# Decay casts on VectorE, half-out projections that open operand by operand, and held blocks evacuated one by one

## The chip, the cores and the metric

The kernel runs on one core of one Trainium2 chip. The metric is the device time of one execution in microseconds (us). The core's engines run side by side, each through its own row of instructions in order, and wait for each other by semaphores: TensorE (PE, matmuls; PEld, its weight loads), VectorE (DVE), ScalarE (ACT), GpSimd (POOL), and SyncE (SP), which issues the loads. [...]

## The reference

Three transformer blocks are applied in sequence to one input x of 512 positions and 1024 features, all in fp32. Cut to what matters here:

```python
x = first_block(x, ...)    # norm, mLSTM and differential attention, out projection, FFN, gated PLE, norm
x = second_block(x, ...)   # stick_breaking_layer, then mla_layer
x = third_block(x, c, ...) # swiglu, hybrid_mixer, swiglu; each modulated by c

# first block
x = x + mixed @ w_out
# second block
return x + (o * jax.nn.silu(gate)) @ w_out       # stick breaking: l0_w_out
# third block
mod = (jax.nn.silu(c) @ w_ada[l] + b_ada[l]).reshape(b_, N_SUB, 3, D_MODEL)
h = modulate(x, norm_pre_g[l, 0], shift[:, 0], scale[:, 0])
h = swiglu(h, ffn_w_gate[l, 0], ffn_w_up[l, 0], ffn_w_down[l, 0])
x = x + 0.5 * (1 + gate[:, 0, None, :]) * rms_norm_3(h, norm_post_g[l, 0])
```

The mLSTM's gates give cumulated decays, in rows of 4 heads by 512 positions. The hybrid mixer's forgetting attention has a cumulated log gate as well, in rows of 8 heads (cs below).

## The kernel before

All activations are held feature-major, as eight tiles X of 128 features by 512 positions. A matmul's fp32 operands are split into a high part (a cast to fp32r: hi, or wh for a weight) and a low part (lo, wl: the value less the high part), and a product is three matmuls: hi with wh, lo with wh, hi with wl. For a weight, load() issues a DMA of 128x1024 into one of three raw buffers, ScalarE casts wh and VectorE subtracts wl. A projection of one 128-feature block over 1024 features, in proj() and mm(), is 24 matmuls of 128x512 into one PSUM bank (tile pm).

The order of the instructions on each engine is decided when the kernel is built, by a scheduler with a cost model; the code's own order is its input. TensorE is in order like the others.

Five places matter here.

*Decays.* In the first block, decays(sb) makes, for each of the four 128-position blocks, a cumulated gate G, a column tile cc and a split tile R of the range from that block to the end, 512 to 128 columns wide. The split is made by parts(): a MEMSET of the tile, the high part in one group of rows (L408, a cast by ScalarE) and the low part in another (L409, VectorE). The calls for the last two blocks stand in the code behind values("w1_mv"), whose projections are token-major matmuls of 128x256 (mm_tok, L439 to L441), evicted by ScalarE as tiles vt (L816). columns() then transposes the four cc on TensorE (tile cps). In the hybrid mixer the same parts() splits cs, which TensorE multiplies into cumb (L1624).

*Half-out projections.* out_half() projects eight blocks and adds half of each to X; it is called with w_out1 in the first block (403 to 452 us) and with w_l0o in the stick-breaking layer (1161 to 1210 us). Here each block is a proj(), and the column sum of the next norm follows at the end.

*Lead.* lead() opens several banks at once: for each operand k, it issues the three matmuls of every bank. The blocks are left in self.ready, from where proj() takes them. The kernel before uses it at the head of other stages, in two halves of 256 columns each.

*Background steps.* The third block's modulation vector is made in 72 steps; each loads a 128x1024 weight into a raw buffer (adaw) and reduces it by one VectorE operation (L1403). proj() starts one at every second call that it counts:

```python
        if (name, i) in self.ready:
            return self.ready.pop((name, i))
        self.count += 1
        if self.count % 2 == 0:
            self.background()
```

ada_finish(), at the end of the mla layer, ahead of its output projection w_l1o, issues all that are left.

*Held blocks.* out_units() makes an output projection of eight blocks, two to a unit. With held=2 the last two units are held back: their banks are made in two turns, for the columns 0 to 255 and 256 to 511, so that a turn's norm (column sum, rc on GpSimd, broadcast bc) can run beside the other turn's matmuls. A bank pm holds two blocks of 256 columns, c = 0 and 1. evac is what takes a block out: in the mla X gets half of it added (L1363, VectorE); in a swiglu's second half H gets it added (L1495, VectorE); in the hybrid mixer ScalarE copies it (L1665). Each then squares it (sq, ScalarE, L254) and sums the squares (acc, VectorE, L258), and the column sum (colsum, L560) reads acc. Four stages end so: the mla, the two swiglus and the hybrid mixer.

Of the kernel before, what the change touches and what calls it, by code (L numbers as in the profile page):

```python
# [20 lines left out]
ALL = slice(0, S)  # L21
# [265 lines left out]
class Net:  # L287
# [116 lines left out]
    def parts(self, out, src, n, sl=ALL):  # L404

        nc = self.nc
        nc.vector.memset(out.bitcast(F32)[:, sl], 0.0)
        nc.scalar.copy(out[0:n, sl], src[0:n, sl])  # L408
        nc.vector.tensor_tensor(out[64:64 + n, sl], src[0:n, sl], out[0:n, sl].bitcast(F32), ALU.subtract)  # L409

    def load(self, name, u, kc, g):
# [74 lines left out]
    def out_units(self, units, x, evac, held=0, turn=None, ahead=None, skip=0):  # L486


        def part(w, j, c, o, sl, n):
            wj, kc = w  # L490
            xs = [(h[:, sl], l[:, sl]) for h, l in x[4 * j:4 * j + kc]]
            self.mm(o, wj, c * P, xs, start=j == 0, stop=j == n - 1)

        def load(piece):
            name, i, kc = piece
            return self.load(name, i, kc, 256), kc

        n = len(units) - held
        two = range(skip, skip + 2) if n - skip >= 2 else range(0)
        if two:  # L500
            J = len(units[skip])
            self.wide, wide = True, self.wide
            ps = {}
            for js in (range(J - 1), range(J - 1, J)):
                for u in two:
                    ws = {j: load(units[u][j]) for j in js}
                    for c in range(2):
                        if (u, c) not in ps:
                            ps[u, c] = self.psm()
                        for j in js:  # L510
                            part(ws[j], j, c, ps[u, c], ALL, J)
                        if J - 1 in js:
                            evac(2 * u + c, ps[u, c], ALL)
            self.wide = wide
        for u in range(skip + len(two), n):
            w = [load(p) for p in units[u]]
            for c in range(2):
                ps = self.psm()
                for j in range(len(w)):
                    part(w[j], j, c, ps, ALL, len(w))  # L520
                evac(2 * u + c, ps, ALL)
        if held == 0:
            return
        ws = [[load(p) for p in units[u]] for u in range(n, n + held)]
        for th, sl in enumerate(HALVES):
            for a, w in enumerate(ws):
                ps = self.psm()
                for c in range(2):
                    for j in range(len(w)):
                        part(w[j], j, c, ps[:, 256 * c:256 * c + 256], sl, len(w))  # L530
                for c in range(2):
                    evac(2 * (n + a) + c, ps[:, 256 * c:256 * c + 256], sl)
            turn(th)
            if ahead is not None and th == 0:
                with self.tc.issue_after(self.dve.ins):
                    ahead()
# [509 lines left out]

    def out_half(self, name, y, norm=None):

        for i in range(8):
            ps = self.proj(name, i, y)  # L1050
            self.nc.vector.scalar_tensor_tensor(self.X[i], ps, 0.5, self.X[i], ALU.mult, ALU.add)
            if norm is not None:
                norm.add(i, self.X[i])
# [382 lines left out]
    def turn(self, s, H, hn, th, nxt, x, done):  # L1436

        nc, sl = self.nc, HALVES[th]
        n = S // 2
        rb = hn.rows(sl, "po")[:, :n]  # L1440
        for k in range(8):
            h, X = H[k][:, sl], self.X[k][:, sl]
            nc.vector.scalar_tensor_tensor(h, h, self.P3[:, 8 * s + k:8 * s + k + 1], rb, ALU.mult, ALU.mult)  # L1443
            if k % 2:
                nc.gpsimd.tensor_tensor(X, X, h, ALU.add)
            else:
                self.dve = nc.vector.tensor_tensor(X, X, h, ALU.add)
            if nxt is not None:
                nxt.add_pe(k, self.X[k], sl)
            else:  # L1450
                done(k, sl)
        if nxt is not None:
            self.enter(s + 1, nxt, th, x)
# [358 lines left out]
```

## Time and profile before

| | us |
|---|---|
| median of 3 runs | 2478.08 |
| lowest and highest of them | 2474.18, 2478.57 |
| the profiled execution's own time | 2473.0 |
| its span, first to last instruction | 2471.1 |
| TensorE busy in the span | 2406.2 (97%) |
| VectorE busy | 1324.0 (54%) |
| ScalarE busy | 991.8 (40%) |
| GpSimd busy | 64.2 (3%) |

Busy time of TensorE is the modelled time of its matmuls. The span lies 1.9 us under the execution's time; what is outside it is start and end. The mean granted clock is 0.989. The DMA queues moved 240.77 MB, 97 GB/s over the span. In the profile's rows, "idle before <- X" means that the engine stood still before the instruction and that X ended last of what it waited for.

### The profile page before, as it was taken

Reading aid. Unit: us, or ns where it says so; the run is one execution under the profiler, and the core shown is the slowest. Engines: PE = TensorE matmul, PEld = TensorE weight load, DVE = VectorE, ACT = ScalarE, POOL = GpSimd, SP = SyncE. Lnnn points to the kernel's source line nnn. Section 1 sums busy time; section 2 is a strip of 40 time slices with the busy share of each in tenths; the row PEclk is TensorE's granted clock in tenths of the full one; section 3 lists DMA queues with packets and bytes.
Section 4 is the critical chain, followed back from the end, with each engine's and each line's share of the span. In section 5 each row is a group of like instructions: output and inputs, shape, how many; then the busy total and the mean of one; then the engine's idle time right before and its main releaser. Section 6 shows DMA issues by size and latency. Waiting matters only on the chain. (4 is left out here: it accounts for less than half of the span.)

```text
span 2471.1 us, 31023 instructions
## 1 busy us (share of the span) xinstructions
PE 2406.2 (97%) x12462; PEld 1980.4 (80%) x12462; DVE 1324.0 (54%) x2240; ACT 991.8 (40%) x1579; POOL 64.2 (3%) x62
## 2 busy tenths in 40 slices
PE   8999999999999999999999999999999999999998
PEld 6877778888888787777877798888898768888887
DVE  7536557684675664446556863323364565432333
ACT  5423433442343545665334643232245444322221
POOL 0000000000000000000000000000010002000001
PEclk9999999999999999999999999999999999999999
DMA  5223235433433432222301323232222211223221
GB/s 190 94 91 98 90 103 179 136 126 105 160 118 115 136 113 76 69 77 77 115 20 63 109 88 111 88 105 98 86 77 78 90 36 60 94 88 109 94 94 44
DMA packets 71745, 240.77 MB, mean 97 GB/s; under 512 B 8232, under 2 KB 11184, under 8 KB 71600
## 3 DMA queue, kind: packets, MB, share of 16 engines
q1 hardware_dynamic: 71600, 238.78, 29.3%
q8 instruction: 98, 1.61, 0.3%
q14 instruction: 47, 0.39, 0.0%
HBM read 236.64 MB, written 2.11 MB: 97 GB/s over the span
## 5 line engine op out<-in xcount | busy, mean ns | idle before, releaser
L429 PE MATMUL pm<-hi,wh 128*128 128x512 f32 (+1 forms) x2736 | 1043.4, 382 | 8.5 <-ACT hi L393 4.7
L430 PE MATMUL pm<-lo,wh 128*128 128x512 f32 (+1 forms) x2736 | 1041.4, 381 | 0.5 <-DVE lo L394 0.4
L431 PE MATMUL pm<-hi,wl 128*128 128x512 f32 (+1 forms) x2736 | 1039.0, 380 | 0.0
L419 ACT CAST wh<-raw 128x1024 fp32r<-128x1024 f32 (+1 forms) x372 | 381.8, 1029 | 781.5 <-PE pm L430 536.2
L420 DVE TENSOR_TENSOR wl<-raw,wh 128x1024 fp32r<-128x1024 f32 (+1 forms) x372 | 445.3, 1197 | 442.2 <-ACT wh L419 417.5
L429 PEld LDWEIGHTS pm<-hi,wh 128*128 128x128 f32 x2736 | 516.2, 189 | 108.4 <-issue 7.9
L430 PEld LDWEIGHTS pm<-lo,wh 128*128 128x128 f32 x2736 | 516.2, 189 | 97.6 <-issue 3.7
L431 PEld LDWEIGHTS pm<-hi,wl 128*128 128x128 f32 x2736 | 516.1, 189 | 96.1 <-issue 3.0
L439 PE MATMUL pm<-wh,hi 128*128 128x256 f32 x400 | 115.7, 289 | 4.9 <-ACT vt L816 4.9
L1403 DVE CUSTOM_DVE_ANT_0 adaw<-adaw,cb 128x1024 f32<-128x1024 f32 x72 | 87.9, 1221 | 54.2 <-DMA adaw<-in_w_ada 54.1
L441 PE MATMUL pm<-wh,lo 128*128 128x256 f32 x400 | 114.4, 286 | 0.0
L440 PE MATMUL pm<-wl,hi 128*128 128x256 f32 x400 | 114.0, 285 | 0.0
L1482 DVE TENSOR_TENSOR sg<-sg,pm 128x512 f32<-128x512 f32 x44 | 30.2, 687 | 133.3 <-PE pm L431 133.3
L572 POOL TENSOR_TENSOR rc<-ms,nhalf 128x4 f32<-128x4 f32 (+2 forms) x29 | 39.3, 1356 | 2309.6 <-DVE ms L577 1863.8
L439 PEld LDWEIGHTS pm<-wh,hi 128*128 128x128 f32 x400 | 77.6, 194 | 5.9 <-ACT vt L816 5.4
L440 PEld LDWEIGHTS pm<-wl,hi 128*128 128x128 f32 x400 | 77.6, 194 | 0.6 <-issue 0.2
L441 PEld LDWEIGHTS pm<-wh,lo 128*128 128x128 f32 x400 | 77.5, 194 | 0.2
L970 DVE SCALAR_TENSOR_TENSOR uy<-ur,vec,uy 128x511 f32<-128x511 f32 x88 | 65.8, 749 | 9.1 <-ACT uy L968 8.0
L481 PE MATMUL pm<-hi,wh 128*128 128x256 f32 (+1 forms) x216 | 61.4, 308 | 9.2 <-ACT hi L400 6.8
L258 DVE TENSOR_TENSOR acc<-acc,sq 128x512 f32<-128x512 f32 (+1 forms) x93 | 54.9, 596 | 24.2 <-ACT sq L254 23.0
L482 PE MATMUL pm<-lo,wh 128*128 128x256 f32 (+1 forms) x216 | 66.1, 308 | 0.3 <-DVE lo L1434 0.3
L483 PE MATMUL pm<-hi,wl 128*128 128x256 f32 (+1 forms) x216 | 66.0, 307 | 0.0
(353 smaller groups left out, 2351.4 us busy)
## 6 DMA issues: line engine op xcount, KB each, us to landing
raw<-in_w_gu SPq DMA_DIRECT2D x88, 512.0 KB, 3.3
adaw<-in_w_ada SPq DMA_DIRECT2D x72, 512.0 KB, 3.3
raw<-in_w_dn SPq DMA_DIRECT2D x48, 512.0 KB, 3.2
raw<-in_w_up SPq DMA_DIRECT2D x44, 512.0 KB, 3.3
raw<-in_w_g SPq DMA_DIRECT2D x16, 512.0 KB, 3.2
raw<-in_w_l0qk SPq DMA_DIRECT2D x16, 512.0 KB, 3.4
raw<-in_w_l SPq DMA_DIRECT2D x12, 512.0 KB, 3.3
X<-in_x SPq DMA_DIRECT2D x16, 256.0 KB, 5.2
```

The source lines that it names most:

```text
L419: nc.scalar.copy(wh[:, :n], raw[:, :n])
L420: nc.vector.tensor_tensor(wl[:, :n], raw[:, :n], wh[:, :n].bitcast(F32), ALU.subtract)
L429: self.nc.tensor.matmul(out, a, xh, start=start and k == 0, stop=False)
L430: self.nc.tensor.matmul(out, a, xl, start=False, stop=False)
L431: self.pe = self.nc.tensor.matmul(out, b, xh, start=False, stop=stop and k == n - 1)
L439: self.nc.tensor.matmul(out, xh[:, sl], a, start=start and k == 0, stop=False)
L440: self.nc.tensor.matmul(out, xh[:, sl], b, start=False, stop=False)
L441: self.pe = self.nc.tensor.matmul(out, xl[:, sl], a, start=False, stop=stop and k == len(x) - 1)
L482: self.nc.tensor.matmul(o[:, sl], wh[:, k], xl[:, sl], start=False, stop=False)
L483: self.nc.tensor.matmul(o[:, sl], wl[:, k], xh[:, sl], start=False, stop=k == 7)
L970: nc.vector.scalar_tensor_tensor(y[:, sh:], raw[:, :S - sh], self.v("fconv_w", 44 * (2 - sh) + f), y[:, sh:], mult, add)
L1403: nc.vector.tensor_tensor_reduce(w, w, cb, 0.5, 0.0, ALU.mult, ALU.add, mod[:, i:i + 1])
```

## The change

Three edits. parts() makes the high part by a VectorE copy instead of a ScalarE copy. out_half() first opens four of its eight blocks by lead(), over all 512 columns, with self.wide set so that psm() may also take banks of the role "sc"; the loop then finds them in self.ready. out_units() takes out each held block right behind its matmuls, ahead of the matmuls of the bank's other block.

```diff
@@ -405,7 +405,7 @@
         nc = self.nc
         nc.vector.memset(out.bitcast(F32)[:, sl], 0.0)
-        nc.scalar.copy(out[0:n, sl], src[0:n, sl])
+        nc.vector.tensor_copy(out[0:n, sl], src[0:n, sl])
         nc.vector.tensor_tensor(out[64:64 + n, sl], src[0:n, sl], out[0:n, sl].bitcast(F32), ALU.subtract)
@@ -528,7 +528,6 @@
                 for c in range(2):
                     for j in range(len(w)):
                         part(w[j], j, c, ps[:, 256 * c:256 * c + 256], sl, len(w))
-                for c in range(2):
                     evac(2 * (n + a) + c, ps[:, 256 * c:256 * c + 256], sl)
@@ -1046,6 +1045,9 @@
     def out_half(self, name, y, norm=None):
 
+        self.wide = True
+        self.lead([(name, i) for i in range(4)], y, parts=[ALL])
+        self.wide = False
         for i in range(8):
             ps = self.proj(name, i, y)
             self.nc.vector.scalar_tensor_tensor(self.X[i], ps, 0.5, self.X[i], ALU.mult, ALU.add)
```

The instructions stand in another order on several engines. On ScalarE, in the first block, where the casts of R and the evictions vt of the first two token-major banks stand (cth is the tanh of the last convolved tile), the order before is:

```order
60 L690 ACTIVATE cth_595<-cy_590 128x512
61 L408 CAST R_611<-G_607 4x512
62 L816 ACTIVATE vt_625<-pm_629,rc_322 128x256
63 L816 ACTIVATE vt_626<-pm_629,rc_322 128x256
64 L408 CAST R_620<-G_616 4x384
65 L816 ACTIVATE vt_627<-pm_630,rc_322 128x256
66 L816 ACTIVATE vt_628<-pm_630,rc_322 128x256
```

and with the change (lines of the code are shifted by one):

```order
60 L689 ACTIVATE cth_595<-cy_590 128x512
61 L815 ACTIVATE vt_625<-pm_629,rc_322 128x256
62 L815 ACTIVATE vt_626<-pm_629,rc_322 128x256
63 L815 ACTIVATE vt_627<-pm_630,rc_322 128x256
64 L815 ACTIVATE vt_628<-pm_630,rc_322 128x256
```

The four evictions stand directly behind the tanh. The casts stand on VectorE, which makes the last ones and the weight's wl behind them:

```order
120 L664 TENSOR_TENSOR cc<-ig,G 4x128
121 L409 TENSOR_TENSOR R<-G,R 4x256
122 L667 TENSOR_TENSOR G<-G,m 4x128
123 L407 MEMSET R 128x128
124 L408 CAST R<-G 4x128
125 L409 TENSOR_TENSOR R<-G,R 4x128
126 L420 TENSOR_TENSOR wl<-raw,wh 128x1024
```

On SP's queue, at the end of the mla layer, the loads of the background steps (adaw) and of the output projection (in_w_l1o) stand before as

```order
210 L416 DMA raw<-in_w_l 128x1024
211 L1402 DMA adaw<-in_w_ada 128x1024 x6
212 L416 DMA raw<-in_w_l1o 128x1024 x8
213 L416 DMA raw<-in_w_gu 128x1024 x22
```

and with the change as

```order
202 L416 DMA raw<-in_w_l 128x1024
203 L1404 DMA adaw<-in_w_ada 128x1024 x10
204 L416 DMA raw<-in_w_l1o 128x1024 x8
205 L416 DMA raw<-in_w_gu 128x1024 x22
```

Four loads more stand ahead of the output projection's. On VectorE, at the end of the kernel, the last turn of the held blocks (x2 is two blocks) stands before as

```order
2055 L1495 TENSOR_TENSOR H<-pm,H 128x256 x2
2056 L258 TENSOR_TENSOR acc<-acc,sq 128x256 x2
2057 L1495 TENSOR_TENSOR H<-pm,H 128x256 x2
2058 L258 TENSOR_TENSOR acc<-acc,sq 128x256 x2
2059 L577 TENSOR_SCALAR ms<-colsum 128x2
```

and with the change as

```order
2078 L1497 TENSOR_TENSOR H<-pm,H 128x256 x2
2079 L258 TENSOR_TENSOR acc<-acc,sq 128x256
2080 L1497 TENSOR_TENSOR H<-pm,H 128x256
2081 L258 TENSOR_TENSOR acc<-acc,sq 128x256 x2
2082 L1497 TENSOR_TENSOR H<-pm,H 128x256
2083 L258 TENSOR_TENSOR acc<-acc,sq 128x256
2084 L576 TENSOR_SCALAR ms<-colsum 128x2
```

One block's H and acc stand last instead of two.

## Rows read from the trace of the kernel before

**Rows 1.** The page: busy time of engines; granted clock in 40 slices.

```profile
PE 2406.2 (97%) x12462; PEld 1980.4 (80%) x12462; DVE 1324.0 (54%) x2240; ACT 991.8 (40%) x1579; POOL 64.2 (3%) x62
...
PEclk9999999999999999999999999999999999999999
```

**Rows 2.** TensorE's waits, whole span: us in total, times, longest.

```profile
PE bc L584 <- POOL rc L572: 20.3, 20, 2.7
...
PE pm L439 <- ACT vt L816: 4.9, 1, 4.9
PE pm L429 <- ACT hi L393: 4.7, 2, 3.4
PE colsum L560 <- DVE acc L258: 2.3, 2, 2.1
...
PE cumb L1624 <- DVE cs L409: 1.6, 1, 1.6
```

**Rows 3.** Windows: from:to, length, busy us (instructions) by engine, clock, DMA.

```profile
34.00:37.00 3.00, 0.96 (x5) 0.49 (x4) 3.00 (x5) 0.43 (x1) 0.00 (x0) 1.00 0.66 217
81.40:86.31 4.91, 0.00 (x1) 0.00 (x1) 4.79 (x10) 1.41 (x4) 0.00 (x0) 0.75 0.46 167
86.31:90.65 4.34, 4.34 (x20) 4.34 (x21) 3.67 (x9) 2.15 (x6) 0.00 (x0) 0.50 0.00 0
403.50:451.60 48.10, 48.10 (x214) 39.56 (x212) 33.76 (x46) 19.60 (x26) 0.00 (x0) 1.00 0.55 187
1162.00:1166.00 4.00, 3.58 (x10) 2.42 (x9) 4.00 (x8) 2.52 (x6) 0.00 (x0) 0.57 0.00 0
1166.00:1210.00 44.00, 44.00 (x196) 36.41 (x195) 34.51 (x50) 21.23 (x31) 0.00 (x0) 1.00 0.35 111
1388.00:1427.00 39.00, 38.72 (x215) 30.78 (x214) 37.34 (x86) 26.02 (x51) 0.00 (x0) 1.00 0.50 163
1444.00:1452.00 8.00, 8.00 (x69) 8.00 (x68) 1.82 (x5) 0.75 (x2) 0.00 (x0) 1.00 0.01 2
```

**Rows 4.** Timeline, ScalarE, 81 to 95.5: start, length, instruction [idle before].

```profile
84.91 0.62 ACT L408 CAST R<-G 4x512 fp32r<-4x512 f32 x1 [3.44 <-DVE G L668]
85.44 0.82 ACT L816 ACTIVATE vt<-pm,rc 128x256 f32<-128x256 f32 x2
```

**Rows 5.** Timeline, VectorE, 81 to 95.5.

```profile
83.85 0.48 DVE L407 MEMSET R<- 128x512 f32 x1
...
86.09 0.68 DVE L409 TENSOR_TENSOR R<-G,R 4x512 fp32r<-4x512 f32 x1
...
88.31 0.55 DVE L409 TENSOR_TENSOR R<-G,R 4x384 fp32r<-4x384 f32 x1 [0.58 <-ACT R L408]
...
90.78 0.28 DVE L665 TENSOR_TENSOR cc<-ig,G 4x128 f32<-4x128 f32 x1
...
92.32 0.28 DVE L409 TENSOR_TENSOR R<-G,R 4x128 fp32r<-4x128 f32 x1 [0.36 <-ACT R L408]
93.90 1.23 DVE L420 TENSOR_TENSOR wl<-raw,wh 128x1024 fp32r<-128x1024 f32 x1 [1.30 <-ACT wh L419]
```

**Rows 6.** Timeline, TensorE, 94.1 to 95.6.

```profile
95.41 0.68 PE L439 MATMUL pm<-wh,hi 128*128 128x256 f32 x1
```

**Rows 7.** Timeline, VectorE, 1393 to 1428.

```profile
1406.92 1.21 DVE L1403 CUSTOM_DVE_ANT_0 adaw<-adaw,cb 128x1024 f32<-128x1024 f32 x1
...
1412.10 1.23 DVE L420 TENSOR_TENSOR wl<-raw,wh 128x1024 fp32r<-128x1024 f32 x1 [1.27 <-ACT wh L419]
```

**Rows 8.** Timeline, ScalarE, 1408 to 1414.

```profile
1411.02 1.05 ACT L419 CAST wh<-raw 128x1024 fp32r<-128x1024 f32 x1 [0.88 <-DMA raw<-in_w_l1o]
```

**Rows 9.** Timeline, all engines, the end of the kernel.

```profile
2457.59 0.76 DVE L1495 TENSOR_TENSOR H<-pm,H 128x256 f32<-128x256 f32 x2 [5.99 <-PE pm L431]
2458.11 0.79 ACT L254 ACTIVATE sq<-H 128x256 f32<-128x256 f32 x2 [7.17 <-DVE H L1495]
2458.56 0.96 DVE L258 TENSOR_TENSOR acc<-acc,sq 128x256 f32<-128x256 f32 x2 [0.21 <-ACT sq L254]
...
2459.66 0.98 PE L560 MATMUL colsum<-ones,acc 128*128 128x1 f32 x4 [2.11 <-DVE acc L258]
```


## Prediction

> **What bounds the kernel now.** I read the page first: TensorE is busy 2406.2 of 2471.1 us at a granted clock that is near full in every slice [rows 1]. Only its gaps and its stretches at half clock can be won, and only new gaps can be lost. The list of its waits [rows 2] says whose gaps they are: 20 waits of the broadcast of a row norm for GpSimd (20.3 us), one of 4.9 us for the eviction vt, two for a split operand (4.7 us), the column sums for VectorE's acc (2.3 us), and one for the decay tile cs (1.6 us). Then windows around the places that the diff touches [rows 3], with timelines inside four of them [rows 4 to 9]. A 128x512 matmul takes 44.00/196 = 0.224 us there, a 128x256 one 8.00/69 = 0.116 us.
>
> The clock needs a word. The gap of 4.91 us at 81.40 is followed by 4.34 us at clock 0.50, which cost about 4.34/2 = 2.2 us; the gap before 1162 is followed by a stretch that averages 0.57; the gap at 34 to 37 us, with TensorE busy 0.96 of 3.00 us, keeps clock 1.00 [rows 3]. So a shifted gap may win or lose a slow stretch. From those rows I put 1.7 to 2.2 us on each.
>
> **Part 1, decays by VectorE.** In the first block ScalarE meets the cast of R at 84.91 after 3.44 us of waiting for VectorE's G, and the evictions vt stand behind it, at 85.44 [rows 4]. TensorE has filled its banks and stands from 81.40 to 86.31. The order of the changed kernel has no such cast: vt follows the last tanh, so its first pair can run from 81.5 and TensorE resumes near 82.4, and the 48 matmuls of two banks, at 0.116 us, are done at 88.0. Before, 20 of them run at half clock to 90.65 [rows 3], and 28 more end at 93.9.
>
> That gain does not arrive whole. TensorE's next work is the transposes of the decay columns, and the next projection needs the split weight wl; both stand behind VectorE, which now also casts. The last cc comes at 90.78 to 91.06, and the wl at 93.90 to 95.13 [rows 5]; the projection that reads it starts at 95.41 [rows 6]. Today that wl waits for ScalarE; in the new order R's last subtraction, ending today at 92.60, sets it. VectorE saves its waits for the casts, 0.58 + 0.36 = 0.94, and takes on four casts. No row shows a VectorE cast of this shape; the nearest are a MEMSET of 512 columns (0.48, about 0.41 as it is spaced) and the subtraction of the same tile (0.68) [rows 5]. Scaled to 512, 384, 256 and 128 columns the sum is 1.23 to 1.94 us. So R ends between 92.60 - 0.94 + 1.23 = 92.9 and 93.6, wl 1.23 later between 94.1 and 94.85, and the projection starts 0.6 to 1.3 us earlier. I take **0.9 gained**, the middle: a copy reads one tile, more than a MEMSET and less than the subtraction. A remaining slow clock would take up to 1.7 of it.
>
> [...]
>
> In the third block the same helper makes cs, which TensorE waits for 1.6 us [rows 2]. The cast moves from ScalarE, where it lay beside VectorE's fqk, into VectorE's row between two fqk: the subtraction comes one cast later, 0.41 to 0.68 us by the same two rows, **0.45 lost**, wholly on the path.
>
> **Part 2, the lead of four blocks.** The first half-out projection has no gap: 48.10 of 48.10 us busy [rows 3]. Its matmuls are the same in number and size, so the order inside gains **0**. At the second one TensorE waits 3.4 of the 4.7 us for the first operand hi [rows 2], behind sigmoid, product and cast. Four blocks operand by operand need the first operand at the same moment. The scheduler interleaves three blocks there already (0.224 x 9 = 2.0 us of work for each operand), and the window after it is full, 44.00 of 44.00 [rows 3]: **0** again. At both ends the last block's addition to X still stands last.
>
> The lead has a hidden part. proj returns a led block before it counts it, and every second count starts one background step (a load on SP's queue into a raw buffer, then a custom VectorE operation). Four blocks less are counted in each of two calls, so four steps move to ada_finish at the end of the second block: SP's row has ten instead of six there, right before the w_l1o weights. One step takes VectorE 1.21 us [rows 7], four 4.8 us. Behind them wait the wl of the output projection, and SP's loads wait for buffers that the steps free; ScalarE already waits 0.88 for such a load, and VectorE 1.27 for its cast [rows 7, 8]. The ends are 0 (TensorE waits for no weight there now: 38.72 of 39.00 us busy) and 4.8. VectorE is idle 39.00 - 37.34 = 1.66 us in this window [rows 3], which absorbs a third; of the other 3.1 I put half on the path, as the first products need two of four weights and the rest have a block of matmuls ahead of them: **1.6 lost**.
>
> **Part 3, held blocks taken out one by one.** Four stages end on two blocks of two 256-column halves. At the end of the kernel, two evictions H, two squares and two acc stand in a row after the last matmul, and the column sum starts 2.11 us after it [rows 9]. Taken out one by one, only one of each is left there. The two acc take 0.96 us, so the end of the chain is one acc, **0.5 us**, earlier, and the end of the kernel with it. The mla and the two inner stages have the same tail before a broadcast wait, with matmuls of a next block behind it to cover part: 0.3 for mla, 0.3 for the other two together. Against it: the two halves lie in one bank and one tile, and the second half's first matmul now waits for the first half's eviction. The nearest row is H: 0.76 us for two, started 0.04 after the last matmul's end (2459.66 - 2.11 = 2457.55) [rows 9], so some 0.46 us with its hand-off. The scheduler puts five matmuls of the other block between, 5 x 0.116 = 0.58, or a whole half of 33. That covers it while VectorE is free. Sum **1.1 gained** (bounds: 1.6 gained, 2 lost).
>
> [...]
>
> **Sum.** -0.9 + 0.45 + 0 + 1.6 - 1.1 = +0.05 us on the profiled execution's 2473.0 (span 2471.1 and 1.9 around it). That execution is 5.1 us below the median of the runs shown, 2478.1, and 1.2 below the lowest of them; I carry the sum to the median: **2478.0 us**. Some 0.2%, 5 us, is what a measurement of this kernel tells from no change.
>
> **Rivals.**
> - *Faster: the stall at 81.40 goes with its slow clock.* If the VectorE chain behind it is shorter than I have it, or the transposes can wait behind other matmuls, the 48 matmuls end 93.9 - 88.0 = 5.9 us earlier and all of it stays. With part 3, cs and half of the backlog: 2478.1 - 5.9 - 1.1 + 0.45 + 0.8 = 2472.4; with a slow stretch less, 2470.7. For it: the 4.91 us and 4.34 slow us are in one place. Against it: cc at 90.78 and wl at 93.90 [rows 5]. Chance 0.18.
> - *Slower: the backlog at ada_finish falls on TensorE whole.* 4.8 instead of 1.6, and one or two slow stretches of 1.7 behind it: 2478.1 + 3.2 + 1.7 = 2483.0, with two 2484.7. It decides when the second weight of w_l1o arrives after the last gate product, for then each further step delays TensorE by 1.2. For it: VectorE is busy 37.34 of 39.00 us in the window [rows 3]. Chance 0.14.
> - *Slower: second halves wait.* Four stages, two turns and two blocks make 16 second halves. Where VectorE is inside a wl operation (1.23 us [rows 5]) the eviction starts up to 1.2 later; if that is the rule, 16 x (0.46 + 0.6 - 0.58) = 7.7 less the 1.1: about 2485. Chance 0.05.
> - *Nothing moves that counts*: TensorE is busy 97% and each part is covered: 2478 too. Chance 0.10.
>
> **How the numbers follow.** My forecast has 0.43 and its own range is 2473 to 2483, which is the sum with the bounds of part 1 and 3 and one or two slow stretches either way. The remaining 0.10 is luck of the clock beyond that, both signs alike. Faster by over 5 us: 0.18 + 0.05 = 0.23; slower: 0.14 + 0.05 + 0.05 = 0.24; same: 0.43 + 0.10 = 0.53. The range takes in the first two rivals with one slow stretch more: 2469 to 2486.
>
> **What would show it.** Right: TensorE's wait for vt is about 1 us instead of 4.9, with a new wait of 3 to 4 us for cc or wl before 95 us; cumb waits about 2.0 for cs; ten background steps before w_l1o and waits of about 1.6 us for wh or wl at 1418 to 1428; the last column sum waits about 1.6 instead of 2.11. Wrong: no stall at 88 to 95 (the first rival), several us of waiting for weights at 1418 (the second), waits of matmuls L429 for H or X in held stages (the third), or a number of slow stretches that differs by three or more.

## The result, and the profile after

The changed kernel takes 2493.28 us (median of 4 runs, 2492.30 to 2498.16) against 2476.98 for the kernel before (4 runs, 2474.18 to 2478.57): 1.0067 times as long, with an interval of 1.0055 to 1.0079. It is slower by some 16 us, outside the range that was given and past its slower end. The profiled execution took 2492.3 us.

The page of the changed kernel: its span, the busy times, and the granted clock in 40 slices.

```profile
span 2490.3 us, 31016 instructions
...
PE 2421.6 (97%) x12462; PEld 1991.1 (80%) x12462; DVE 1324.6 (53%) x2245; ACT 991.1 (40%) x1574; POOL 64.9 (3%) x62
...
PEclk9999999999999999999999999999989999999999
```

TensorE issues the same 12462 matmuls as before [rows 1] and is busy 15.4 us longer with them (2421.6 - 2406.2). The span grew by 19.2 us, so only 3.8 us are new idle time; the rest is the same work at a lower clock. The mean granted clock of the two profiled executions says the same: 0.982 after, 0.989 before. Taken in windows of 1 us, the granted clock of TensorE is 1.00 in 2408 of the 2471 windows before, 0.50 in 44 and between the two in 19; after, it is 1.00 in 2393 of 2490, 0.50 in 77 and between in 20. So I estimate the time at half clock as 2 x (1 - clock) x span: 89.7 us after and 54.4 before. A 128x256 matmul takes 4.34/20 = 0.217 us at clock 0.50 [rows 3], against 0.116 at 1.00. Half of the 35 us between them, 17.6 us, is then an upper bound of what it cost, as a gap at half clock costs nothing. A part of the 35 us is luck of the traced execution: the four runs of the changed kernel come to 75 to 95 us at half clock (median 87), 35 runs of the kernel before to 49 to 84 (median 64). One slice, the thirtieth, now shows an 8. The question is therefore which 3.8 us of gaps stand where so much half clock came in.

TensorE's waits in the changed kernel: us in total, times, longest.

```profile
PE bc L583 <- POOL rc L571: 20.1, 19, 2.3
...
PE colsum L559 <- DVE acc L258: 4.7, 3, 1.7
PE cps L675 <- DVE cc L664: 2.5, 2, 1.5
PE colsum L268 <- ACT sq L264: 2.3, 2, 1.7
...
PE cumb L1626 <- DVE cs L409: 1.7, 1, 1.7
...
PE pm L429 <- ACT wh L419: 1.2, 2, 0.9
...
PE pm L439 <- ACT vt L815: 0.8, 1, 0.8
...
PE pm L431 <- DVE wl L420: 0.4, 1, 0.4
...
PE pm L429 <- DVE X L1365: 0.2, 1, 0.2
```

Against [rows 2]: the wait for vt fell from 4.9 to 0.8, with a new one of 2.5 for cc; the wait of the column sums for acc doubled, from 2.3 to 4.7; and column sums now wait for a square, too. That is a small list, and no line of it is worth 16 us.

So I compared the starts of the n-th matmul of both traces, TensorE being in order and their number equal. The places where the distance jumps are few (my own comparison of the two traces, us):

```
matmul   before     after    later by
   360    79.32     79.97      0.65
   600   119.30    118.34     -0.96    first block, decays: 1.6 won
  2100   445.12    444.21     -0.91
  2160   458.24    462.01      3.77    end of the first half-out projection: 4.7 lost
  8750  1796.00   1805.85      9.85    between: several small steps, below
  9250  1861.15   1879.27     18.13    end of the first swiglu: 8.3 lost
 12440  2455.71   2475.89     20.17
 12461  2462.48   2481.61     19.13    end of the kernel: 1.0 won back
```

**First place, 449 to 461 us.** VectorE at the end of the first half-out projection, in the changed kernel (start, length, instruction, idle before it):

```profile
446.01 1.22 DVE L420 TENSOR_TENSOR wl<-raw,wh 128x1024 fp32r<-128x1024 f32 x1 [0.33 <-ACT wh L419]
447.15 1.22 DVE L1405 CUSTOM_DVE_ANT_0 adaw<-adaw,cb 128x1024 f32<-128x1024 f32 x1
...
448.30 0.68 DVE L1053 SCALAR_TENSOR_TENSOR X<-pm,X 128x512 f32<-128x512 f32 x1
449.21 1.23 DVE L420 TENSOR_TENSOR wl<-raw,wh 128x1024 fp32r<-128x1024 f32 x1 [0.23 <-ACT wh L419]
...
451.01 0.69 DVE L258 TENSOR_TENSOR acc<-acc,sq 128x512 f32<-128x512 f32 x1
452.91 0.16 DVE L576 TENSOR_SCALAR ms<-colsum 128x4 f32<-128x4 f32 x1 [1.21 <-PE colsum L559]
452.99 1.22 DVE L1405 CUSTOM_DVE_ANT_0 adaw<-adaw,cb 128x1024 f32<-128x1024 f32 x1
```

The same place in the kernel before:

```profile
447.21 1.22 DVE L1403 CUSTOM_DVE_ANT_0 adaw<-adaw,cb 128x1024 f32<-128x1024 f32 x1 [2.17 <-DMA adaw<-in_w_ada]
...
448.36 0.69 DVE L1051 SCALAR_TENSOR_TENSOR X<-pm,X 128x512 f32<-128x512 f32 x1
448.96 1.22 DVE L420 TENSOR_TENSOR wl<-raw,wh 128x1024 fp32r<-128x1024 f32 x1
...
450.76 0.68 DVE L258 TENSOR_TENSOR acc<-acc,sq 128x512 f32<-128x512 f32 x1
```

The cast wh that the changed kernel's last wl waits for:

```profile
448.13 1.05 ACT L419 CAST wh<-raw 128x1024 fp32r<-128x1024 f32 x1 [2.15 <-DMA raw<-in_w_up]
```

GpSimd's rc, in the changed kernel and then in the kernel before:

```profile
453.21 1.85 POOL L571 TENSOR_TENSOR rc<-ms,nhalf 128x4 f32<-128x4 f32 x1 [113.17 <-DVE ms L576]
```

```profile
452.96 1.01 POOL L572 TENSOR_TENSOR rc<-ms,nhalf 128x4 f32<-128x4 f32 x1 [111.88 <-DVE ms L577]
```

TensorE comes here 0.9 us early, but X and acc don't: acc starts at 451.01 instead of 450.76. In both kernels a background step stands directly ahead of the last X and a weight wl behind it. Before, VectorE had stood idle for 2.17 us ahead of that step, whose load came late. In the changed kernel one wl more stands in that place and waits for its own cast, the step starts at nearly the same time (447.15 instead of 447.21), and the wl behind X waits 0.23 us for a cast that had waited 2.15 us for its load. TensorE has done its matmuls at 450.49 and stands 1.36 us for acc, where it stood for nothing before. And a second background step now stands right behind ms, where the kernel before has no operation until 455.21, so it runs at the same time as rc, which takes 1.85 us instead of 1.01, and the broadcast waits 1.68 us instead of 0.83. TensorE has only two matmuls between these gaps, and then runs mostly at half clock (a mean of 0.56 over 456 to 461 us). Windows of the changed kernel at both places (from:to, length, busy us and instructions by engine, clock, DMA share, GB/s):

```profile
449.00:456.00 7.00, 3.96 (x21) 2.98 (x20) 3.79 (x6) 1.32 (x3) 1.85 (x1) 0.82 0.66 229
456.00:461.00 5.00, 5.00 (x17) 4.16 (x17) 3.18 (x4) 1.86 (x2) 0.00 (x0) 0.56 0.15 61
...
1846.00:1853.00 7.00, 5.11 (x37) 4.33 (x36) 5.12 (x11) 3.33 (x5) 1.60 (x1) 1.00 0.63 202
1853.00:1867.00 14.00, 12.27 (x57) 11.98 (x58) 9.72 (x23) 5.54 (x13) 4.24 (x5) 0.51 0.17 57
```

**Second place, 1841 to 1867 us.** Windows of the kernel before at the same work:

```profile
1836.00:1848.00 12.00, 11.38 (x98) 11.17 (x96) 10.53 (x27) 6.06 (x15) 4.58 (x6) 1.00 0.10 39
1848.00:1862.00 14.00, 12.73 (x91) 12.20 (x91) 9.13 (x19) 6.17 (x12) 0.57 (x1) 0.88 0.24 76
```

Before, 98 matmuls fill 11.38 of 12 us beside the norm; after, 37 fill 5.11 of 7, and what follows runs at clock 0.51. The reason lies earlier, in the loads of the next stage's weights. SP's row in the kernel before, and then in the changed one, from the third of the four loads in_w_qk on (the first two are issued ahead of the norm in both):

```profile
1823.63 2.63 SPq L416 DMA_DIRECT2D raw<-in_w_qk  x2
```

```profile
1841.65 1.86 SPq L416 DMA_DIRECT2D raw<-in_w_qk  x2
```

ScalarE in the changed kernel from the first squares of that turn's norm on:

```profile
1828.95 0.96 ACT L264 ACTIVATE sq<-X 128x256 f32<-128x256 f32 x2 [4.26 <-DVE X L1449]
...
1839.31 1.05 ACT L419 CAST wh<-raw 128x1024 fp32r<-128x1024 f32 x1 [3.95 <-PE pm L430]
...
1844.91 1.05 ACT L419 CAST wh<-raw 128x1024 fp32r<-128x1024 f32 x1 [0.60 <-DMA raw<-in_w_qk]
```

and the same two steps in the kernel before:

```profile
1818.67 0.95 ACT L264 ACTIVATE sq<-X 128x256 f32<-128x256 f32 x2 [4.46 <-DVE X L1447]
...
1821.28 1.05 ACT L419 CAST wh<-raw 128x1024 fp32r<-128x1024 f32 x1 [0.55 <-PE pm L430]
```

Counted from those first squares, the next cast wh comes after 10.4 us instead of 2.6, and SP's next load after 12.7 instead of 5.0. The cast waits for a buffer, and the buffer for the matmul L430 that reads its old weight. In the changed kernel the second half of a bank (its second block) waits for the eviction of the first half (the list above has one such wait, 0.2 us for X; the run that forbids the order by halves, below, has eight, of 0.46 to 3.6 us), so in the second turn the two banks are done by halves: first half of one, first half of the other, second half of the one, second half of the other. The weights of both banks are then in use almost to the end of the stage, where before the first bank gave its buffers back earlier: the cast waits for the 9006th matmul instead of the 8945th. The next stage's weights come late: between the broadcast and the next column sums TensorE has three matmuls to do, where it had 17. The two rows of TensorE on which this ends, in the changed kernel:

```profile
1851.58 0.71 PE L583 MATMUL bc<-cst,rc 128*128 128x128 f32 x4 [1.47 <-POOL rc L571]
...
1854.37 3.78 PE L268 MATMUL colsum<-ones,sq 128*128 128x1 f32 x17 [1.73 <-ACT sq L264]
```

The wait of 1.47 us for rc has a cause of its own: a wl of the late weights now starts 0.16 us ahead of rc, which takes 1.60 us instead of 0.87. VectorE and GpSimd in the changed kernel, then GpSimd in the kernel before:

```profile
1849.76 1.21 DVE L420 TENSOR_TENSOR wl<-raw,wh 128x1024 fp32r<-128x1024 f32 x1
```

```profile
1849.92 1.60 POOL L571 TENSOR_TENSOR rc<-ms,nhalf 128x2 f32<-128x2 f32 x1 [11.88 <-DVE ms L576]
```

```profile
1838.80 0.87 POOL L572 TENSOR_TENSOR rc<-ms,nhalf 128x2 f32<-128x2 f32 x1 [10.49 <-DVE ms L577]
```

In all, TensorE's waits at this place are 4.6 us instead of 1.5, and its stretch at half clock is 13.7 us instead of 3.4, which is up to 5.2 us of time. Together they make the 8.3.

### The profile page after: what moved, and what is told of

Same layout as the page of the kernel before. It is cut to its first block, busy times and chain, and to the rows that moved or that the text cites. A ratio compares the mean times of both kernels' runs of the same rounds, so it can differ in the third digit from the quotient of the medians.

```text
span 2490.3 us, 31016 instructions
## 1 busy us (share of the span) xinstructions
PE 2421.6 (97%) x12462; PEld 1991.1 (80%) x12462; DVE 1324.6 (53%) x2245; ACT 991.1 (40%) x1574; POOL 64.9 (3%) x62
## 3 DMA queue, kind: packets, MB, share of 16 engines
HBM read 236.64 MB, written 2.11 MB: 96 GB/s over the span
## 5 line engine op out<-in xcount | busy, mean ns | idle before, releaser
L429 PE MATMUL pm<-hi,wh 128*128 128x512 f32 (+1 forms) x2672 | 1021.4, 383 | 6.4 <-DVE cr L683 2.0
L430 PE MATMUL pm<-lo,wh 128*128 128x512 f32 (+1 forms) x2672 | 1016.2, 380 | 0.0
L431 PE MATMUL pm<-hi,wl 128*128 128x512 f32 (+1 forms) x2672 | 1012.4, 380 | 0.4 <-DVE wl L420 0.4
L429 PEld LDWEIGHTS pm<-hi,wh 128*128 128x128 f32 x2672 | 504.3, 189 | 104.8 <-issue 7.9
L430 PEld LDWEIGHTS pm<-lo,wh 128*128 128x128 f32 x2672 | 504.4, 189 | 93.7 <-issue 3.7
L431 PEld LDWEIGHTS pm<-hi,wl 128*128 128x128 f32 x2672 | 503.7, 189 | 94.3 <-issue 3.0
L571 POOL TENSOR_TENSOR rc<-ms,nhalf 128x4 f32<-128x4 f32 (+2 forms) x29 | 40.1, 1381 | 2325.1 <-DVE ms L576 1890.0
L481 PE MATMUL pm<-hi,wh 128*128 128x256 f32 (+1 forms) x280 | 86.8, 332 | 12.9 <-ACT hi L400 6.9
L482 PE MATMUL pm<-lo,wh 128*128 128x256 f32 (+1 forms) x280 | 92.6, 333 | 0.0
L483 PE MATMUL pm<-hi,wl 128*128 128x256 f32 (+1 forms) x280 | 91.9, 330 | 0.0
```

The costliest lines, as they stand in the source:

```text
L429: self.nc.tensor.matmul(out, a, xh, start=start and k == 0, stop=False)
L430: self.nc.tensor.matmul(out, a, xl, start=False, stop=False)
L431: self.pe = self.nc.tensor.matmul(out, b, xh, start=False, stop=stop and k == n - 1)
L481: self.nc.tensor.matmul(o[:, sl], wh[:, k], xh[:, sl], start=k == 0, stop=False)
L482: self.nc.tensor.matmul(o[:, sl], wh[:, k], xl[:, sl], start=False, stop=False)
L483: self.nc.tensor.matmul(o[:, sl], wl[:, k], xh[:, sl], start=False, stop=k == 7)
```

## The experiments

All ratios are against the kernel before on the same chip, whose median was 2478.62 us for the next four kernels. First the change was taken apart: the three edits one at a time, and the kernel before once more as a measure of luck.

### The cast alone

```diff
-        nc.scalar.copy(out[0:n, sl], src[0:n, sl])
+        nc.vector.tensor_copy(out[0:n, sl], src[0:n, sl])
```

> The decay casts on VectorE alone, the rest as before. Theory (the loss comes from the order that the other two edits bring, not from the casts): the wait for vt falls from 4.91 to about 0.9, two waits of 1.0 to 1.5 for cc come in, cumb waits 0.1 longer; in sum 1 us faster up to the end of that stage, 2475 to 2478 with luck of the clock. Rival (VectorE is overloaded by the casts and what follows comes late): 2480 or more, with new waits for wl between 90 and 110 us.

2476.51 us, ratio 0.9989 (0.9979 to 1.0). Nothing is lost. Its trace has the waits that were expected (0.9 us for vt, 2.5 in two for cc, 1.7 for cs). The 2.1 us that the median lies lower are no gain that can be told: the kernel before once more, below, lies as much lower.

### The lead alone

```diff
+        self.wide = True
+        self.lead([(name, i) for i in range(4)], y, parts=[ALL])
+        self.wide = False
```

> The lead of four blocks in the half-out projections alone. Theory: at the ends of both projections a background step stands before the last acc and beside rc, which costs 2 to 3 us of gaps and one or two slow stretches at 450 to 460 and about 1 us at 1215; the four steps more at ada_finish cost 1.5; in sum 5 to 9 us slower, 2482 to 2486. Rival (all of the loss is the one-by-one evacuation): 2476 to 2479.

2483.11 us, ratio 1.0019 (1.0008 to 1.0031): some 4.5 us lost. Its trace has the gaps of 1.43 us (column sum for acc) and 1.68 us (broadcast for rc) at 452.7 to 457.4, with rc again at 1.85, and the weight waits of 0.96 and 0.35 us at 1423 to 1431. Its acc starts at 453.27, which is 1.2 us late even against a TensorE that comes 1.3 us later than in the kernel before. The time lies in the range expected, the loss just under the 5 to 9 us.

### One-by-one eviction alone

```diff
                     for j in range(len(w)):
                         part(w[j], j, c, ps[:, 256 * c:256 * c + 256], sl, len(w))
-                for c in range(2):
                     evac(2 * (n + a) + c, ps[:, 256 * c:256 * c + 256], sl)
```

> One-by-one evacuation of the held blocks alone. Theory: the two held banks are filled by turns, so the weights of both stay in use until the end, the next stage's weights are loaded some 18 us later, and TensorE has too few matmuls to lay beside the norm at 1850: gaps of about 3 us there instead of 0.4 and some 10 us more of slow clock; 6 to 9 us slower, 2483 to 2486, although the last column sum comes 0.5 earlier. Rival (the second halves wait for the evictions): many waits of L429 for H or X, 0.2 to 0.5 each, spread over all four stages. Rival (the loss is the lead's): 2475 to 2478.

2486.19 us, ratio 1.0033 (1.0023 to 1.0043): some 7.6 us lost, where a gain had been forecast. SP's next load starts at 1836.70, 12.7 us behind the first squares at 1823.99, as in the changed kernel, and the window of the column sums runs at half clock throughout:

```profile
1848.00:1862.00 14.00, 12.47 (x57) 11.88 (x57) 9.97 (x23) 5.33 (x13) 4.25 (x5) 0.50 0.19 66
```

### The kernel before, once more

> The kernel before once more, for a second trace of it. If the slow stretches between 1290 and 1385, where the order of TensorE is the same in both kernels, are luck of where the gaps fall in time, they differ from those of the first trace (three of 3.4 us) by one or more stretches; if they belong to the program they come back the same. The time is 2474 to 2479 either way.

2476.55 us, ratio 0.9992 (0.998 to 1.0003). Its time is the same within the interval, though the median lies 2.07 us lower: so much is luck in these series. But its half clock isn't in the same places: 10.2 us at 1330 where the first trace has 3.4, and 6.8 at 1289 where that has 3.4. Over 35 runs of the kernel before in one series, the time at half clock went from 49 to 84 us. So a half-clock stretch that one trace shows and another doesn't proves nothing here; the two places above are named because they stand against either trace of the kernel before (4.9 and 8.3 us lost against the second, at the same matmuls).

### A bank for each half

If the loss of the third edit comes from the shared bank, which makes the second half wait and so has the two banks done by halves in turn, it must go when each half has a bank of its own, with the eviction still one by one.

```diff
-                ps = self.psm()
...
                 for c in range(2):
+                    ps = self.psm()
                     for j in range(len(w)):
-                        part(w[j], j, c, ps[:, 256 * c:256 * c + 256], sl, len(w))
-                for c in range(2):
-                    evac(2 * (n + a) + c, ps[:, 256 * c:256 * c + 256], sl)
+                        part(w[j], j, c, ps[:, 0:256], sl, len(w))
+                    evac(2 * (n + a) + c, ps[:, 0:256], sl)
```

> One-by-one evacuation with a bank of its own for each 256-column half, no other edit: a second half waits for no eviction, so one unit is finished before the next begins and its weights are free as early as before. Theory (the loss was the longer life of the held weights): SP loads the next stage's weights between 1820 and 1835 again, the gaps at 1850 shrink from 3 us to under 1, and the early column sum stays; 2474 to 2479, at or a little below the kernel before. Rival (evicting one by one keeps VectorE from the next stage's operands): still 2483 to 2487.

2479.42 us against 2477.58 on this chip, ratio 1.0008 (0.9999 to 1.0018), so most of the 7.6 us is gone. SP's next load and the cast that frees its buffer are within 1 us of where they were, 5.9 and 3.5 us behind the first squares at 1823.57 (SP's row, then ScalarE's, of this kernel):

```profile
1829.44 2.20 SPq L416 DMA_DIRECT2D raw<-in_w_qk  x2
```

```profile
1827.11 1.05 ACT L419 CAST wh<-raw 128x1024 fp32r<-128x1024 f32 x1 [1.47 <-PE pm L430]
```

The broadcasts' waits at 1845 and 1856 are 0.51 and 0.67 us, under 1 as expected, and no half waits for an eviction. But not all is mended: in the three traces with a bank for each half (this one, the slowest of its ten runs, and the two under "Both causes mended") the place from the 8750th to the 9250th matmul still loses 4.0, 3.6 and 2.5 us, with 6.8 to 10.2 us at half clock. What that rest is, no run settles.

### The shared bank, but block after block

The rival cure: keep one bank for both halves and forbid the order by halves, so that each half starts only behind the one made before it, and the first bank's weights are free early.

```diff
-                    for j in range(len(w)):
-                        part(w[j], j, c, ps[:, 256 * c:256 * c + 256], sl, len(w))
-                for c in range(2):
+                    if a or c:
+                        with self.tc.issue_after(self.pe.ins):
+                            for j in range(len(w)):
+                                part(w[j], j, c, ps[:, 256 * c:256 * c + 256], sl, len(w))
...
                     evac(2 * (n + a) + c, ps[:, 256 * c:256 * c + 256], sl)
```

> One-by-one evacuation with one bank for two halves as in the change, but the second bank's matmuls held behind the first bank's by an order constraint, so that a second half mostly follows its own first half at once. Theory (life of the weights): the loads come early again and the loss at 1850 goes, but up to 12 second halves wait about 0.5 us each for an eviction; 2478 to 2485. Rival of the prediction (uncovered second halves are the cost): each waits 0.5 or more and the time is 2485 to 2489, no better than the one-by-one edit alone. If the order at 1850 alone counts, 2476 to 2479.

2497.95 us, ratio 1.0098 (1.0083 to 1.0113): slower than any other kernel here, and not what was expected. The waits that the order by halves had covered now lie open:

```profile
PE pm L429 <- DVE H L1499: 5.1, 4, 3.6
```

with 1.9 us more in three waits for ScalarE's H and 0.5 in one for X: eight waits, 7.5 us. That is the price that the order by halves saves. Six of the eight are 0.46 to 0.52 us each, which is the 0.46 that I had put on one; the wait of 3.6 us, at 2469 us, stands where VectorE comes to the eviction only at 2468.49, behind its work for the other turn's norm. With a bank for each half, above, TensorE's list has no such wait.

The weights come free only in part earlier: the cast waits for the 8973rd matmul, against the 9006th with the change and the 8945th before, and SP's next load starts at 1835.77, 11.6 us behind the first squares. Even so the norm is covered again: TensorE has 23 matmuls between the broadcast and the next column sums, the broadcast waits 0.45 us, and from the 9000th to the 9600th matmul it loses 2.2 us, where the one-by-one edit alone loses 8.2. So the loss at 1850 did mostly go, as the theory of this run has it, and the time is lost elsewhere: of the 20.4 us, 7.5 are the waits at the halves, and the four runs come to 80 to 90 us at half clock (median 87, the kernel before on this chip 64), which is up to some 12 us.

### The led blocks counted

Four background steps had moved to the end of the mla layer, since led blocks return before they are counted. Here they count.

```diff
-        if (name, i) in self.ready:
+        led = (name, i) in self.ready
+        if not led or name in ("w_out1", "w_l0o"):
+            self.count += 1
+            if self.count % 2 == 0:
+                self.background()
+        if led:
             return self.ready.pop((name, i))
-        self.count += 1
-        if self.count % 2 == 0:
-            self.background()
```

(with the lead as above.)

> The lead of four blocks alone, but led blocks are counted, so that the background steps stay as many before ada_finish as they were. If the four steps more at ada_finish cost what the trace shows, the waits for wh and wl after 1420 (0.96 and 0.35) go and the time is 1.0 to 1.6 below that of the lead alone, 2481 to 2482; the gaps at 452 to 457 stay, since a step still stands there. If the shifted steps were the whole loss of the lead, 2477 to 2479.

2483.35 us against 2477.58, ratio 1.0031 (1.002 to 1.0043). The weight waits at 1423 to 1431 are gone, as expected, but the gaps of 1.64 and 1.68 us at 452 to 457 are still there, and so is the loss; the 1.0 to 1.6 us less that were expected don't show. The backlog was not what the lead lost.

### A VectorE operation beside rc

If rc is longer only because VectorE works beside it, a single added operation behind each ms must lengthen it in the kernel before, too. This kernel does one operation more for each norm, whose result nobody reads.

```diff
-        return net.rpow(net.ms_eps(ps, self.n, n), n)
+        ms = net.ms_eps(ps, self.n, n)
+        z = net.q(F32, "beside")
+        net.nc.vector.scalar_tensor_tensor(z, net.cst[:, 0:S], ms[:, 0:1], net.cst[:, 256:256 + S], ALU.mult, ALU.add)
+        return net.rpow(ms, n)
```

> The kernel before with one VectorE operation more (two fp32 tiles of 512 columns, 0.69 us) right behind ms in each norm, so beside GpSimd's rc; its result is used nowhere. If VectorE's use of SBUF holds GpSimd up, the four-column rc of 1.0 us becomes 1.4 to 1.6, the two-column one of 0.8 becomes 1.3, the sum of bc's waits for rc grows by 5 to 9 us, and the time by 5 to 12 with slow stretches. Rival (rc is long for a reason of its own, as at 823): rc stays at 1.0 and 0.8 where it was, and the time within 3 us.

2488.23 us against 2477.58, ratio 1.0053 (1.0038 to 1.0068). The added operation and rc at the first half-out projection's end:

```profile
456.10 0.75 DVE L277 SCALAR_TENSOR_TENSOR beside<-cst,ms 128x512 f32<-128x512 f32 x1
```

```profile
456.20 1.51 POOL L575 TENSOR_TENSOR rc<-ms,nhalf 128x4 f32<-128x4 f32 x1 [111.87 <-DVE ms L580]
```

rc ends at 457.71, 0.86 us behind the end of the operation at 456.85. In the changed kernel it ends at 455.06, 0.85 us behind the background step's end at 454.21. In both, rc ends equally long behind VectorE's operation, though that takes 0.75 us here and 1.22 there. That it is VectorE's use of SBUF that holds rc up was my supposition; the times do not show it. The total of the broadcast waits did not grow with it (20.3 us, the kernel before has 20.3); they grew at some norms (0.83 to 1.33 us at 456 and 1216) and shrank at others, where another order came out. So this run shows the length of rc, and not cleanly what it costs. The time grew by 10.7 us, inside the 5 to 12 expected, but not through the sum of waits that was to bring it; in the traces TensorE is busy 11.6 us longer with the same matmuls (2417.8 against 2406.2) at a mean granted clock of 0.985 against 0.989, so most of it is clock.

### Where in the lead the loss lies

The lead at the second half-out projection only:

```diff
+        self.wide = True
+        if name == "w_l0o":
+            self.lead([(name, i) for i in range(4)], y, parts=[ALL])
+        self.wide = False
```

> The lead in the second half-out projection alone (w_l0o). Theory (of the lead's loss most lies at the first projection's end): the gaps at 450 to 457 are those of the kernel before (0.83), two steps more at ada_finish, 2478 to 2481. Rival (most lies behind the second projection): 2482 to 2485.

2478.12 us against 2477.36, ratio 1.0003 (0.9994 to 1.0013). And the lead at both, with the background steps of w_out1 and of the first eight w_up1 projections moved behind them, so that none stands beside the end of the first half-out projection or the norm behind it:

```diff
-        if self.count % 2 == 0:
+        if name == "w_up1" and 8 <= i < 32:
+            self.background()
+        elif self.count % 2 == 0 and name != "w_out1" and not (name == "w_up1" and i < 8):
             self.background()
```

> The lead of four blocks alone, with the background steps of the first half-out projection and of the first eight projections behind it moved to the later projections of the same block. Theory (at 450 to 457 a background step stands before the last X and another beside rc): the gaps there, 1.4 and 1.7 us, shrink to at most 0.9 together with the slow stretch behind them, rc takes 1.0 again instead of 1.85, and the time is 2478 to 2481. Rival (the lead itself delays the last block's chain, by the order of its banks): the gap before the column sum stays at 1.4 and the time at 2482 to 2485.

2478.26 us against 2477.36, ratio 1.0005 (0.9996 to 1.0015), and 1.0019 for the lead as it was. VectorE, then GpSimd, then the windows of this kernel at the place:

```profile
447.43 0.69 DVE L1056 SCALAR_TENSOR_TENSOR X<-pm,X 128x512 f32<-128x512 f32 x1 [2.09 <-PE pm L431]
```

```profile
452.29 1.01 POOL L574 TENSOR_TENSOR rc<-ms,nhalf 128x4 f32<-128x4 f32 x1 [111.01 <-DVE ms L579]
```

```profile
447.00:454.00 7.00, 6.17 (x33) 4.84 (x32) 3.34 (x5) 2.20 (x3) 1.01 (x1) 1.00 0.23 81
454.00:459.00 5.00, 5.00 (x26) 4.19 (x25) 4.42 (x7) 1.88 (x2) 0.00 (x0) 1.00 0.30 97
```

X starts when TensorE lets it, rc takes 1.01 us, the column sum waits for nothing, and the clock stays at 1.00. The lead itself costs nothing that can be told; what stood around it did. The run moves both steps at once, so it doesn't say how much either cost alone, and the steps were not moved in the kernel before, without the lead.

### Both causes mended

The cast with a bank for each half, without the lead:

> Casts on VectorE and one-by-one evacuation with a bank for each half, without the lead. If the two edits add up and nothing of the held weights' longer life is left, 2475 to 2479: no measurable difference, at best 2 us below the kernel before. If evacuating one by one costs something else than the life of the weights, 2482 or more.

2480.14 us against 2477.36, ratio 1.001 (1.0 to 1.0019): between the two ranges expected, so it decides for neither. And all three edits with both cures, a bank for each half and the moved background steps (the diffs of the sections above together):

> All three edits, with a bank for each half and with the background steps moved as in the lead's experiment. If the two causes named (longer life of the held weights, background steps in the norm's chain) make up the whole loss, 2476 to 2481; if a good part is something else, 2484 or more.

2478.77 us, ratio 1.0008 (0.9997 to 1.0018). The three edits as they came cost 1.0067; with these two causes taken away, there is nothing that can be told from the kernel before. At the first place the lateness is now 1.04 us ahead of it and 1.08 behind it (the 1800th and the 2400th matmul), at the second -0.22 and 2.43 (the 9000th and the 9600th): the first is mended whole, the second for the most part. No version was measurably faster than the kernel before.

## Why the prediction was wrong, point by point

**Part 1, right in kind, its size partly luck.** The wait for vt is 0.8 us, as I wrote, and the new wait for cc 2.5 instead of 3 to 4. The place won 1.6 us in this trace and not 0.9. The casts are on record now (line L408 of the changed kernel, mean ns of one):

```profile
L408 DVE CAST R<-G 4x512 fp32r<-4x512 f32 x1 | 0.4, 387 | 0.0
...
L408 DVE CAST R<-G 4x384 fp32r<-4x384 f32 x1 | 0.3, 348 | 0.0
...
L408 DVE CAST R<-G 4x256 fp32r<-4x256 f32 x1 | 0.3, 256 | 0.0
...
L408 DVE CAST R<-G 4x128 fp32r<-4x128 f32 x1 | 0.2, 215 | 0.0
```

Their sum is 1.21 us, just under the 1.23 to 1.94 that I had from a MEMSET and a subtraction. From 128 to 512 columns a cast grows by 172 ns, 0.45 ns a column, where the subtraction of the same tile takes 1.04 (0.28 to 0.68 us, [rows 5]). By the same rows some 0.16 us of each cast (0.215 - 128 x 0.00045) don't grow with its columns.

The 1.6 is in large part clock: in the run of the cast alone, where the half-clock stretch kept its 6.8 us (3.4 in the changed kernel), the same place won 0.5 (0.28 late at the 360th matmul, 0.19 early at the 600th). My 0.9 also had a slip in it. I counted from the end of wl in the new order to 95.41, the start of a matmul that waits for nothing [rows 6]; against wl's own end, 95.13, the same sum gives 0.3 to 1.0. In the changed kernel wl ends at 94.53, 0.6 earlier.

For cs the loss was 0.1 us (1.7 against 1.6), not 0.45. The cast took 0.40 us, as I had it, and from the start of the scan cum to the subtraction it is 3.25 us instead of 2.92, but TensorE's wait grew by only 0.1; where the rest went I did not follow.

**Part 2, the step that failed first.** "Its matmuls are the same in number and size, so the order inside gains **0**" holds; the run with moved steps shows it. "At both ends the last block's addition to X still stands last" was the wrong half of the sentence. X stands last among the additions, but I had not followed VectorE's row from there to the norm: a step ahead of X and a weight behind it stood there before, too, and the changed order took the idle time that they had in front of them and set a second step behind ms. That cost 4.7 us at one place: 2.2 of gaps (1.36 + 1.68 - 0.83) and the rest at half clock. The second end lost little: its acc waits 1.74 us, behind a step that waits 1.51 us for its own load, and the lead there alone is not measurably slower. The backlog at ada_finish, the 1.6 of the sum, came about as forecast (waits of 0.95 and 0.35 us for wh and wl, and 1.9 us later behind it), but taking it away didn't change the time.

**Part 3, the step that failed most.** "The scheduler puts five matmuls of the other block between ... That covers it" is what happens: the waits of second halves in the list are 0.2 us. But I costed the cover at nothing and did not ask what the order by halves holds on to. It holds the weights of both banks almost to the end of the stage, the next stage's loads start 7.7 us later behind the norm's squares, and the norm's gap lies open: 8.3 us at one of four stages in the trace, 7.6 in the time of the edit alone, instead of 1.1 won in all. The tail at the end of the kernel was right:

```profile
2479.30 0.58 PE L559 MATMUL colsum<-ones,acc 128*128 128x1 f32 x4 [1.58 <-DVE acc L258]
```

1.58 us against 2.11 [rows 9], the 0.5 of the forecast.

**The clock, mis-sized.** I put 1.7 to 2.2 us on a slow stretch, from the one at 86 to 90 us [rows 3]. By the windows of the two places it was at half clock for 6.9 us (2 x (0.18 x 7 + 0.44 x 5)) and 13.7 us (2 x 0.49 x 14), which is up to 3.4 and 6.9 us of time; the first began inside the 7.00 us of which TensorE was busy 3.96, the second right behind the 7.00 with 5.11. I had counted waits that go away and come, one by one; I had not looked for two gaps and a row of one-column matmuls that fall together.

**What stays open.** The two places make 13.0 of the 16 to 19 us (13.2 of 15.7 against the second trace of the kernel before). The three edits alone sum to 10 us (-2.1 + 4.5 + 7.6), some 6 less than the change. But each of the three is taken from the same median of the kernel before, so its error counts three times: from the 2476.55 of the kernel before once more they sum to 16.2 (0.0 + 6.6 + 9.6). So it is not shown that the edits cost more together than apart. Between 830 and 1450 us the change's trace loses 4.7 us more than the first trace of the kernel before (5.02 later at the 3900th matmul, 9.72 at the 7200th), but 1.5 more than the second (4.64 to 6.13, from the 4200th), and the order of TensorE at 1293 to 1381, where most of it lies, is the same. I take that part for luck of the clock; no run settles it.

## What to carry to other kernels

Where one bank serves two halves and is emptied between them, a scheduler that covers the wait with the other bank's work keeps the weights of both banks in use: look at when the next stage's loads start, not only at whether the wait is covered. An edit that leaves all matmuls as they are can still move background work on another engine, so follow that engine's row through the next column sum and norm, which is where TensorE had the least to fall back on here (two matmuls between the gaps at the first place, three at the second). Beside the two norms the new gaps came with as much loss again at half clock, or more (2.2 us of new gaps went with a loss of 4.7, 3.1 with one of 8.3). What one trace shows of that has to be held against a second trace of the same kernel, and a small gain against the kernel before run once more.

## What the runs showed of the hardware

GpSimd's rc of 128x4 takes 1.01 us with VectorE idle (452.96 us, kernel before). It takes 1.51 us where the added operation starts 0.10 us ahead of it, and 1.85 us where a background step starts 0.22 us ahead of it (453.21 us, changed kernel); it ends 0.86 and 0.85 us behind the end of that operation. The kernel before has it, too: at 823.48 and 2036.62 us rc takes 1.85 us, behind a wl that starts 0.23 and 0.25 us ahead of it, and ends 0.86 and 0.87 us behind the wl. I had not expected a 4-column operation to end so late behind a 1024-column one on another engine; why it does is not shown. The other way round, a wl that starts 0.10 us behind an rc of 128x2 (1827.61 us, kernel before) takes 1.22 us, its usual time, and that rc 0.71, as without one (0.69 to 0.71).

The same program, run 35 times, spent between 49 and 84 us at half clock (worked out from the granted clock and the span of each run), and its times lay between 2472.19 and 2482.68 us.
